# Hybrid diffusion layer on one core: one activation table for the attention, gate columns as native strips, other ranks in the written-out order

## The chip, the cores and the metric

The kernel runs on one core of a Trainium2 chip. The number that counts is device microseconds (us) of one launch, as the median of several runs. Four engines compute: TensorE (PE, matrix products into PSUM banks), VectorE (DVE), ScalarE (ACT) and GpSimd (POOL, which here only clears buffers and issues some DMAs). SyncE (SP) issues the other DMAs. Each engine works through its own list of instructions in a fixed order and waits on semaphores.

## The reference

One layer over 256 latent tokens and 256 context tokens of width 2048, all in float32:

```python
hx = _rmsnorm(x, norm1_g) * (1.0 + sc1_x) + sh1_x        # and hc from ctx
zx = hx @ w_in + b_in ; zc = hc @ w_in + b_in            # columns: S5 | conv | q | k | v | o | 16 gates
s5_x = s5_mixer(...)         # diagonal state space model, both directions, gelu, gated by a sigmoid
ml_x = mlstm_mixer(...)      # 4 heads of 256, both directions; gates: log_i, log_sigmoid(f)
cv_x = conv_module(...)      # depthwise convolution of 31 taps, layernorm, silu
x = x + g1_x * (concat([s5_x, cv_x, ml_x]) @ w_out)
hx2 = _rmsnorm(x, norm2_g) * (1.0 + sc2_x) + sh2_x
x = x + g2_x * ((silu(hx2 @ w_g) * (hx2 @ w_u)) @ w_ffn_out)
return _rmsnorm(x, norm_f_g)
```

The shifts, scales and gates (`sh`, `sc`, `g`) come from `silu(c) @ w_mod`, a matrix-vector product over 2048 x 12288 weights. In the attention part, each head and direction needs exponentials of a 256 x 512 block, and the readout needs `1/sqrt(var + eps)` per head, made from a logarithm and an exponential.

## The kernel before

**Weights.** All large matrices stream from memory in chunks of 8 tiles of 128 x 128 (`raw`, 512 KB, issued on SP's queue). Each chunk is split for fp32r products: ScalarE casts it to a high part (`split`: `whi`, line 577), VectorE subtracts to get the low part (`wlo`, line 579). Each of the three buffers has three places. An activation is split the same way (`hx`, `hc`, each with a high and a low half), and a product is three matmuls (`mm3`: high x high, high x low, low x high).

**Stages of TensorE's stream.** S5 and first K columns while the normalised input is made (to about 145 us), conv columns, the 16 gate columns, the other K columns, V columns (two blocks, `cb` 0 and 1, each ending in four additions that take the four PSUM banks to `vx`, line 1358), Q, O, the S5 gate (`glu`), the output projection in two halves, then the feed-forward part. In the V stage a block needs four banks for its whole length, and the three `ps_m` banks are all there are of that kind, so the next stage's first matmul waits for the first addition of the block before.

**Side work.** Generators (`s5_job`, `conv_job`, `mod_job`, `gates_job`, `attention`) are advanced between tiles by a small scheduler, `Sched`, so that their instructions are written between the matmuls. `mod_job` makes the second to last parts of the modulation with 512 KB weight pieces (`wm`) from POOL's queue, mostly as multiply-adds on VectorE (`macc`, line 489), each group of 16 ended by four transposes on TensorE. `s5_moves` (line 1094) copies the S5 columns `zT` into another partition order, `U`, with 8 copies on ScalarE and 8 on VectorE. It is called when the first stage ends.

**The order.** After everything is written, `Arrange` simulates all instructions with costs of its own and lays down a fixed order for each engine: whenever an engine is free it takes, of the instructions that are ready, the one with the lowest rank. A rank is the position in the order of writing, less what `ranks` holds for it (line 320). So rank only decides among instructions that are ready together, and its times are the costs written in `account`, not the chip's. Up to `strict`, TensorE keeps the order of writing.

**Activation tables.** ScalarE holds one table at a time, and a load is put before an activation whose function the table lacks. `lnexp()` (line 622) loads the one that has both logarithm and exponential. It is called for the first norm, the conv norm, the gates and two more norms, and not for the attention. `Arrange` counts Exp and Ln as one table, 1.

**Gates.** `load_gates` (line 662) loads 16 columns for each of 16 row tiles, splits them into high and low (`wgs`, 32 columns), and `gates_job` (line 1271) makes 64 fp32r matmuls that write 32 PSUM partitions. A product with `selg` then adds the high and the low rows and puts each group of four on its own 32 partitions.

Of the kernel before, what the change touches and what calls it, by code (L numbers as in the profile page):

```python
# [39 lines left out]
PUMP_EVERY = 8  # L40
URGENT = 0
S5_Y = (3000, 0, 0, 0)
# [109 lines left out]
class Arrange:  # L152
# [5 lines left out]
           "EngineType.SP": "SP"}  # L158
    SETS = {"Exp": 1, "Ln": 1, "Silu": 2, "Sigmoid": 3, "Sin": 4, "Gelu_apprx_tanh": 5}
    CALM, LATE, LATE_M = 140e3, 800.0, 0.0  # L160
    SEM, SAME, DMA, RATE = 45.0, 36.0, 1900.0, 345.0

# [112 lines left out]
    def account(self, k, i, e, size):  # L275
        n = max([s[0] for s in size] or [0])
        out = [s for s in size if s[4]]
        op, c = i.opcode, 0.0
        scal = sum(1 for x in size[:-1] if x[0] == 1)
        psum = any("_pp_" in self.tag.get(x[1], "") for x in size if not x[4])  # L280
        tab = None
        if op == "DMACopy":
            c = out[0][0] * out[0][3][0][1] * 4 / self.RATE
        elif e == "PE":
            cols = out[0][0]
            f32r = "float32r" in str(size[0][2])
            strip = i.tile_size[1] < 128
            c = 6 + 0.4427 * cols if f32r else 109.0 if i.is_transpose else 2 * max(0.8438 * cols, 110.0)
            if any(x[1].startswith(("whi", "wlo")) for x in size):
                self.main.add(k)  # L290
            self.mm[k] = (strip and not f32r, i.tile_position[1])
        elif e == "DVE":
            text = i.concise()
            c = 150 + (2.0 if "is_tensor_tensor_scan=True" in text else 0.5 if op == "Memset" else 1.05) * n
            c += 60 * scal
        elif op == "LoadActFuncSet":
            tab = 1
        elif e == "ACT":
            text = i.concise() if op == "Activation" else ""
            c = 190 + 0.84 * n + 95 * scal - (40 if op == "TensorCopy" and psum else 0)  # L300
            for f, s in self.SETS.items():
                if f"func=ActivationFunctionType.{f} " in text + " ":
                    tab = s
        else:
            c = 300.0
        self.cost.append(c)
        self.tab.append(tab)

    def run(self):
# [31 lines left out]
        while todo:  # L341
# [46 lines left out]
            if self.ins[k].opcode == "DMACopy":  # L388
                clock[e] = s + (530.0 if e == "POOL" else 60.0)
                pipe = max(s + self.DMA + (1200.0 if e == "POOL" else 0.0), pipe) + c  # L390
                done = pipe
# [15 lines left out]
            else:  # L407
                if self.tab[k] is not None and self.tab[k] != table:
                    table = self.tab[k]
                    s += 1300  # L410
# [42 lines left out]
def hybrid_layer_kernel(ctx: ExitStack, tc: tile.TileContext, xt, ctxt, wm1, wmr, wst, wg, bvrow, pvd, cstd, s5p, out):  # L453
# [20 lines left out]

    def tt(o, a, b, op, first=0):
        i = V.tensor_tensor(out=o, in0=a, in1=b, op=op)  # L476
        if first:
            ranks[i.ins.name] = first
        sc.dve += 62 + 1.05 * n_of(o)

    def ts(o, a, s1, op0, s2=None, op1=None):
# [6 lines left out]
    def stt(o, a, s, b, op0, op1):  # L488
        V.scalar_tensor_tensor(o, a, s, b, op0=op0, op1=op1)  # L489
        sc.dve += 62 + 1.05 * n_of(o)  # L490

    def vcopy(o, a):
        V.tensor_copy(o, a)
        sc.dve += 62 + 0.8 * n_of(o)

    def rsum(o, a):
# [7 lines left out]
    def act(o, a, f, bias=0.0, scale=1.0, pin=False):  # L504
        i = S.activation(o, a, f, bias=bias, scale=scale)  # L505
        if pin:
            keep(i)
        sc.act += 190 + 0.84 * n_of(o)

    def acopy(o, a, first=0):  # L510
        i = S.copy(o, a)  # L511
        if first:
            ranks[i.ins.name] = first
        sc.act += 190 + 0.84 * n_of(o)

    def mm(o, l, r, start, stop, native=False, tp=None, sgc=False, pin=False):
# [58 lines left out]
    def split(c):  # L575
        his[c] = sb.tile([128, CH * 128], F32R, name="whi", tag="whi", bufs=3)
        acopy(his[c], raw[c], URGENT)
        los[c] = sb.tile([128, CH * 128], F32R, name="wlo", tag="wlo", bufs=3)
        tt(los[c], raw[c], his[c], OP.subtract, URGENT)
        for d in (raw, his, los):  # L580
# [77 lines left out]
    for q in range(4):  # L658
        nc.sync.dma_start(cr[:, 4 * q:4 * q + 4, :], ctxt[:, 4 * q:4 * q + 4, :])
    wgs = pre.tile([128, KT, 32], F32R, name="wgs", tag="qh")  # L660

    def load_gates():
        wgr = tmp(256).rearrange("p (k n) -> p k n", k=KT)
        nc.sync.dma_start(wgr, wg)
        acopy(wgs[:, :, 0:16], wgr)
        tt(wgs[:, :, 16:32], wgr, wgs[:, :, 0:16], OP.subtract)

# [287 lines left out]
    csq = XB[:, 16 * ROWP + 1024:16 * ROWP + 2048].rearrange("p (t n) -> p t n", t=4)  # L955
    selg = XB[0:32, 3600:3728]
    nc.gpsimd.dma_start(selg, cstd[0:32, C_SELG:])
    V.memset(gp[:, :, :, 0:CONV_K // 2], 0.0)
# [135 lines left out]
    def s5_moves():  # L1094
        for s in range(4):
            for q in range(4):
                o = U[32 * s:32 * s + 32, q::4, :]
                i = zT[32 * q:32 * q + 32, :, s::4]
                if (s + q) % 2:
                    vcopy(o, i)  # L1100
                else:
                    acopy(o, i)

# [167 lines left out]
    def gates_job():  # L1271
        ps = bbank()
        for i, h in ((0, hx), (1, hc)):
            for kt in range(KT):
                for s in range(2):
                    mm(ps[0:32, 256 * i:256 * i + 256], wgs[:, kt, :], h[:, kt, s, :], kt == 0 and s == 0,
                       kt == KT - 1 and s == 1)
        rows = pre.tile([128, 1024], F32, name="rows", tag="qh")
        e = rows[0:32, 512:1024]
        acopy(e, ps[0:32, :])  # L1280
        yield 1500
# [61 lines left out]
    for cb in range(2):  # L1343
# [13 lines left out]
        for t in range(4):  # L1357
            tt(vx[:, t, 2 * cb:2 * cb + 2, 0:256], pss[t].rearrange("p (h d) -> p h d", h=2),
               bvb.rearrange("p (h d) -> p h d", h=2), OP.add)

# [76 lines left out]

    def attention():
        for h in range(ML_H):
            while st["tile"] < q_ready[h]:  # L1440
# [46 lines left out]
    for ct in range(4):  # L1487
# [3 lines left out]
        sg, f = tmp(256), tmp(256)  # L1491
        act(sg, ps[:, 0:256], AF.Sigmoid, bias=pvc("bglu", ct))
        tt(f, gT[ct // 2][:, ct % 2, :], sg, OP.mult)
        to_mix(mixs[:, ct], f)
    need_mod(0)
    rj = sc.add(readout(), 0)
    for ct in range(KT):
        ps = mbank()
        for i in range(8):
            src, j = (mx["c"], i) if i < 4 else (mixs, i - 4)  # L1500
            mm3(ps[:, 0:256], nxt(), (src[:, j, 0, :], src[:, j, 1, :]), i == 0, i == 7)
        stt(xres[:, ct, :], ps[:, 0:256], mods[:, 0, ct:ct + 1], xres[:, ct, :], OP.mult, OP.add)
    sc.finish(rj)
# [4 lines left out]
    class SumSq:  # L1508
# [7 lines left out]
        def add(self, x):  # L1516
            if self.n % 2 == 0:
                self.t = tmp(512)
            sq = self.t[:, 256 * (self.n % 2):256 * (self.n % 2) + 256]
            act(sq, x, AF.Square)  # L1520
            self.sq.append(sq)
# [17 lines left out]
    for ct in range(KT):  # L1539
        ps = mbank()  # L1540
        for i in range(8):
            mm3(ps[:, 0:256], nxt(), (mixm[:, i, 0, :], mixm[:, i, 1, :]), i == 0, i == 7)
        stt(xres[:, ct, :], ps[:, 0:256], mods[:, 0, ct:ct + 1], xres[:, ct, :], OP.mult, OP.add)
        if ct == 14:
# [98 lines left out]
def pack(inp):  # L1643
# [24 lines left out]
    g = f["w_in"][0][:, OFF_G:][:, gi]  # L1668
    a["wg"] = np.ascontiguousarray(g.reshape(KT, 128, 16).transpose(1, 0, 2))
    bi = f["b_in"][0]  # L1670
# [41 lines left out]
    cst[:, C_MR:C_MR + 128] = np.tril(np.ones((128, 128)))  # L1712
    for r in range(32):
        q = r % 16
# [34 lines left out]
```

## Time and profile before

| | us |
|---|---|
| median of 3 runs | 1461.62 (1460.66 to 1464.09) |
| the profiled execution, its own time | 1460.26 |
| its span, first to last instruction | 1458.5 |
| TensorE busy | 1412.2 (97%) |
| VectorE busy | 1050.6 (72%) |
| ScalarE busy | 751.1 (52%) |
| mean granted TensorE clock | 0.989 of full |

Between the span and the execution's own time lie 1.8 us. Busy matmul time has modelled ends, so 97% doesn't say that TensorE works at its peak. It says that little of the span is left in which it waits for somebody.

### The profile page before, as it was taken

How to read it: one execution, taken by the hardware profiler on the slowest of the kernel's cores; microseconds unless marked ns; L12 is line 12 of the kernel's file. 1: busy time of each engine (PE TensorE's matmuls, PEld its weight loads, DVE VectorE, ACT ScalarE, POOL GpSimd, SP SyncE). 2: the span in 40 equal slices, each digit the busy share in tenths (PEclk: the TensorE clock that was granted, in tenths of full speed). 3: DMA queues.
4: the chain of work that ended last, by engine and by line, in shares of the span. 5: the costliest groups of instructions: out<-in, count | busy, mean ns of one | idle time of the engine just before them, and what ended most of it. 6: DMA issues, size and time to landing. Idle time of an engine off the chain costs nothing.

```text
span 1458.5 us, 25393 instructions
## 1 busy us (share of the span) xinstructions
PE 1412.2 (97%) x9856; PEld 1242.8 (85%) x9856; DVE 1050.6 (72%) x1945; ACT 751.1 (52%) x1311; POOL 108.2 (7%) x207
## 2 busy tenths in 40 slices
PE   6999899999999999999999999999999999999996
PEld 4888788887788999998998888888888888888885
DVE  8555699997878787888877778566555665556665
ACT  5334886665664555545555545533444334444353
POOL 1221111110001001011000010000000000000000
PEclk9999999999999999999999999999999999999998
DMA  9997553453428467689477787555555555555553
GB/s 369 366 356 288 180 204 129 177 190 106 158 73 309 169 239 255 228 303 332 146 252 271 270 297 256 185 189 186 188 188 188 188 186 188 188 188 188 188 174 115
DMA packets 87928, 315.31 MB, mean 216 GB/s; under 512 B 10096, under 2 KB 10880, under 8 KB 87808
## 3 DMA queue, kind: packets, MB, share of 16 engines
q1 hardware_dynamic: 60912, 216.67, 42.9%
q0 software_dynamic: 26896, 97.02, 18.6%
q8 instruction: 77, 1.26, 0.3%
q14 instruction: 43, 0.35, 0.1%
HBM read 311.55 MB, written 2.10 MB: 215 GB/s over the span
## 4 chain that ended last, share of the span: by engine, by line
PE 72%; issue 18%; DMA 4%; DVE 2%; POOL 2%; ACT 1%; SPq 0%; POOLq 0%; DVEq 0%
PE ps_m L520 45%; PE ps_qk L520 19%; PE ps_b L520 8%; DMA wm<-in_wmr_dram 4%; POOL wm L650 1%; DVE tmp L476 0%; ACT U L511 0%; ACT tmp L505 0%; PE ps_b L1163 0%; DVE xres L476 0%; PE ps_b L1070 0%; DMA xr<-in_xt_dram 0%; DVE wlo L476 0%; DVE tmp L489 0%; DVE macc L489 0%
## 5 line engine op out<-in xcount | busy, mean ns | idle before, releaser
L476 DVE TENSOR_TENSOR wlo<-raw,whi 128x1024 fp32r<-128x1024 f32 x386 | 471.7, 1223 | 267.4 <-ACT whi L511 262.4
L511 ACT CAST whi<-raw 128x1024 fp32r<-128x1024 f32 x386 | 403.9, 1047 | 456.5 <-PE ps_m L520 248.1
L520 PE MATMUL ps_m<-h,whi 128*128 128x512 f32 (+1 forms) x800 | 252.4, 369 | 3.5 <-ACT h L505 3.5
L520 PE MATMUL ps_m<-ffa,whi 128*128 128x512 f32 x704 | 249.0, 396 | 0.0
L520 PE MATMUL ps_qk<-h,whi 128*128 128x512 f32 (+1 forms) x688 | 233.0, 383 | 0.0
L520 PE MATMUL ps_m<-h,wlo 128*128 128x256 f32 x704 | 199.8, 284 | 0.0
L520 PE MATMUL ps_m<-ffa,wlo 128*128 128x256 f32 x704 | 198.7, 282 | 0.0
L520 PE MATMUL ps_m<-hx,whi 128*128 128x256 f32 x960 | 187.4, 290 | 6.4 <-ACT hx L505 3.2
L520 PE MATMUL ps_qk<-h,wlo 128*128 128x256 f32 x656 | 185.5, 283 | 0.0
L520 PEld LDWEIGHTS ps_m<-h,whi 128*128 128x128 f32 x800 | 145.1, 190 | 30.4 <-ACT h L505 3.9
L520 PEld LDWEIGHTS ps_m<-hx,whi 128*128 128x128 f32 x960 | 149.4, 190 | 21.5 <-issue 16.5
L520 PEld LDWEIGHTS ps_m<-ffa,whi 128*128 128x128 f32 x704 | 132.3, 188 | 32.2 <-issue 1.2
L520 PEld LDWEIGHTS ps_qk<-h,whi 128*128 128x128 f32 x688 | 127.3, 188 | 27.1
L489 DVE SCALAR_TENSOR_TENSOR macc<-wm,cs,macc 128x512 f32<-128x512 f32 x180 | 134.4, 747 | 11.3 <-DMA wm<-in_wmr_dram 7.4
L520 PE MATMUL ps_m<-hx,wlo 128*128 128x256 f32 x480 | 136.8, 285 | 0.7 <-DVE wlo L476 0.7
L520 PEld LDWEIGHTS ps_m<-h,wlo 128*128 128x128 f32 x704 | 133.2, 189 | 0.0
L520 PEld LDWEIGHTS ps_m<-ffa,wlo 128*128 128x128 f32 x704 | 132.3, 188 | 0.1
L520 PEld LDWEIGHTS ps_qk<-h,wlo 128*128 128x128 f32 x656 | 123.4, 188 | 0.0
L650 POOL DMA_DIRECT2D wm<-in_wmr_dram x128 | 67.8, 531 | 602.9 <-DVE macc L489 428.5
L489 DVE SCALAR_TENSOR_TENSOR xres<-ps_m,mods,xres 128x256 f32<-128x256 f32 x160 | 77.0, 482 | 33.6 <-PE ps_m L520 31.6
L520 PEld LDWEIGHTS ps_m<-hx,wlo 128*128 128x128 f32 x480 | 91.3, 190 | 1.4 <-DVE wlo L476 1.2
L489 DVE SCALAR_TENSOR_TENSOR XB<-XB,pv 128x256 f32<-128x256 f32 x120 | 53.8, 475 | 0.4
(273 smaller groups left out, 2134.2 us busy)
## 6 DMA issues: line engine op xcount, KB each, us to landing
raw<-in_wst_dram SPq DMA_DIRECT2D x386, 512.0 KB, 4.2
wm<-in_wmr_dram POOLq DMA_DIRECT2D x128, 512.0 KB, 5.2
wm<-in_wm_dram POOLq DMA_DIRECT2D x24, 512.0 KB, 7.2
wmu<-in_wm_dram POOLq DMA_DIRECT2D x16, 512.0 KB, 7.3
wmt<-in_wm_dram POOLq DMA_DIRECT2D x8, 512.0 KB, 7.7
wms<-in_wm_dram POOLq DMA_DIRECT2D x7, 512.0 KB, 6.2
xr<-in_xt_dram SPq DMA_DIRECT2D x4, 512.0 KB, 5.7
cr<-in_ctxt_dram SPq DMA_DIRECT2D x4, 512.0 KB, 8.9
```

Of the source, the lines that this page charges most:

```text
L476: i = V.tensor_tensor(out=o, in0=a, in1=b, op=op)
L489: V.scalar_tensor_tensor(o, a, s, b, op0=op0, op1=op1)
L511: i = S.copy(o, a)
L520: i = P.matmul(o, lhsT=l, rhs=r, start=start, stop=stop, skip_group_check=sgc, **kw)
L650: i = (q or nc.gpsimd).dma_start(wm[key], src)
```

## The change

1. **Table.** `attention` calls `lnexp()` at its first step. In `Arrange`, Exp is now known to lie in tables 1 and 7, Ln in 6 and 7, and the preloaded table is 7.
2. **Gates.** `wgs` is loaded as plain float32 with 32 columns, of which 16 are zero, straight into its place. The cast, the subtraction and a temporary buffer go. The 64 matmuls are native float32, in groups of four side by side: each writes its own 32 of 128 PSUM partitions and takes every fourth row tile. `selg` has 128 rows and adds the four strips.
3. **Ranks.** `split` (`U_SPLIT`), the two places with `U_OUT`, and `U_GLU` have 0, which is what they had. `s5_moves` gets -60 (`U_MOVE`): each of the 16 copies ranks as if written 60 instructions later. The `vx` additions get 1000 (`U_V`): as if written 1000 instructions earlier.

```diff
-URGENT = 0
+U_SPLIT, U_MOVE, U_V, U_OUT, U_GLU = (0, -60, 1000, 0, 0)
...
-    SETS = {"Exp": 1, "Ln": 1, "Silu": 2, "Sigmoid": 3, "Sin": 4, "Gelu_apprx_tanh": 5}
+    SETS = {"Exp": (1, 7), "Ln": (6, 7), "Silu": (2,), "Sigmoid": (3,), "Sin": (4,), "Gelu_apprx_tanh": (5,)}
...
-            tab = 1
+            tab = (7,)
...
-                if self.tab[k] is not None and self.tab[k] != table:
-                    table = self.tab[k]
+                if self.tab[k] is not None and table not in self.tab[k]:
+                    table = self.tab[k][0]
                     s += 1300
...
+    def ahead(n, i):
+        ranks[i.ins.name] = n
...
-        acopy(his[c], raw[c], URGENT)
+        ahead(U_SPLIT, acopy(his[c], raw[c]))
...
-    wgs = pre.tile([128, KT, 32], F32R, name="wgs", tag="qh")
+    wgs = pre.tile([128, KT, 32], F32, name="wgs", tag="qh")
 
     def load_gates():
-        wgr = tmp(256).rearrange("p (k n) -> p k n", k=KT)
-        nc.sync.dma_start(wgr, wg)
-        acopy(wgs[:, :, 0:16], wgr)
-        tt(wgs[:, :, 16:32], wgr, wgs[:, :, 0:16], OP.subtract)
+        nc.sync.dma_start(wgs, wg)
...
-    selg = XB[0:32, 3600:3728]
-    nc.gpsimd.dma_start(selg, cstd[0:32, C_SELG:])
+    selg = XB[:, 3600:3728]
+    nc.gpsimd.dma_start(selg, cstd[:, C_SELG:])
...
                 if (s + q) % 2:
-                    vcopy(o, i)
+                    ahead(U_MOVE, vcopy(o, i))
                 else:
-                    acopy(o, i)
+                    ahead(U_MOVE, acopy(o, i))
...
-            for kt in range(KT):
+            for k in range(0, KT, 4):
                 for s in range(2):
-                    mm(ps[0:32, 256 * i:256 * i + 256], wgs[:, kt, :], h[:, kt, s, :], kt == 0 and s == 0,
-                       kt == KT - 1 and s == 1)
+                    for j in range(4):
+                        mm(ps[32 * j:32 * j + 32, 256 * i:256 * i + 256], wgs[:, k + j, :], h[:, k + j, s, :].bitcast(F32),
+                           k + s == 0, k == KT - 4 and s == 1, native=True, tp=(0, 32 * j), pin=i + k + s + j > 0)
         rows = pre.tile([128, 1024], F32, name="rows", tag="qh")
-        e = rows[0:32, 512:1024]
-        acopy(e, ps[0:32, :])
+        e = rows[:, 512:1024]
+        acopy(e, ps)
...
-            tt(vx[:, t, 2 * cb:2 * cb + 2, 0:256], pss[t].rearrange("p (h d) -> p h d", h=2),
-               bvb.rearrange("p (h d) -> p h d", h=2), OP.add)
+            ahead(U_V, tt(vx[:, t, 2 * cb:2 * cb + 2, 0:256], pss[t].rearrange("p (h d) -> p h d", h=2),
+                          bvb.rearrange("p (h d) -> p h d", h=2), OP.add))
...
     def attention():
+        lnexp()
         for h in range(ML_H):
```

## Rows read from the trace of the kernel before

**Rows 1.** The page's first part: busy us, share of the span, instructions.
```profile
PE 1412.2 (97%) x9856; PEld 1242.8 (85%) x9856; DVE 1050.6 (72%) x1945; ACT 751.1 (52%) x1311; POOL 108.2 (7%) x207
```

**Rows 2.** Waits of TensorE, whole span: total us, times, longest us.
```profile
PE ps_m L520 <- DVE vx L476: 5.1, 2, 3.2
```

**Rows 3.** Stretches: length, busy us by engine, granted TensorE clock (PEclk), DMA.
```profile
156.10:160.30 4.20, 3.62 (x18) 3.39 (x19) 3.60 (x4) 4.16 (x10) 0.00 (x0) 0.59 0.40 124
...
380.70:385.20 4.50, 4.45 (x21) 3.92 (x21) 4.37 (x9) 4.06 (x13) 0.00 (x0) 0.65 0.13 32
...
443.30:447.10 3.80, 3.80 (x22) 3.80 (x21) 3.80 (x6) 0.80 (x1) 0.53 (x1) 0.55 0.63 221
...
450.00:575.00 125.00, 125.00 (x882) 117.05 (x882) 98.58 (x232) 68.31 (x135) 12.72 (x24) 1.00 0.67 232
```

**Rows 4.** ScalarE in order of time at the S5 copies: start, us.
```profile
145.90 1.25 ACT L505 ACTIVATE kT<-ps_b,bks 128x512 f32<-128x512 f32 x2
147.16 7.86 ACT L511 COPY U<-zT 32x512 f32<-32x512 f32 x7
155.04 1.99 ACT L511 CAST whi<-raw 128x1024 fp32r<-128x1024 f32 x2
```

**Rows 5.** TensorE in order of time, same place.
```profile
151.63 0.40 PE L520 MATMUL ps_b<-hx,whi 128*128 128x256 f32 x2
...
151.99 0.40 PE L520 MATMUL ps_b<-hx,whi 128*128 128x256 f32 x2
...
156.14 0.50 PE L520 MATMUL ps_b<-hx,whi 128*128 128x256 f32 x2 [3.64 <-ACT whi L511]
...
157.40 0.58 PE L520 MATMUL ps_b<-hx,wlo 128*128 128x256 f32 x1 [0.54 <-DVE wlo L476]
```

**Rows 6.** VectorE, end of the first V block.
```profile
380.00 0.69 DVE L476 TENSOR_TENSOR vx<-ps_m,bvb 128x512 f32<-128x512 f32 x1
```

**Rows 7.** TensorE, end of the first V block.
```profile
376.35 0.62 PE L520 MATMUL ps_m<-whi,hx 128*128 128x512 f32 x2
...
380.75 0.51 PE L520 MATMUL ps_m<-whi,hx 128*128 128x512 f32 x1 [1.91 <-DVE vx L476]
```

**Rows 8.** VectorE, end of the second V block.
```profile
437.57 1.22 DVE L476 TENSOR_TENSOR wlo<-raw,whi 128x1024 fp32r<-128x1024 f32 x1
439.86 1.54 DVE L489 SCALAR_TENSOR_TENSOR macc<-wm,cs,macc 128x512 f32<-128x512 f32 x2 [1.06 <-DMA wm<-in_wmr_dram]
441.31 1.28 DVE L476 TENSOR_TENSOR vx<-ps_m,bvb 128x512 f32<-128x512 f32 x2
```

**Rows 9.** TensorE, end of the second V block.
```profile
442.14 0.47 PE L520 MATMUL ps_m<-hx,whi 128*128 128x256 f32 x2 [3.17 <-DVE vx L476]
```

**Rows 10.** TensorE: the gate matmuls, and strips of the first stage's modulation.
```profile
96.08 0.64 PE L520 MATMUL ps_b<-wmt,cs 128*32 128x256 f32 x8
...
96.97 1.05 PE L520 MATMUL ps_b<-wm,cs 128*32 128x256 f32 x16
...
220.79 3.80 PE L520 MATMUL ps_b<-hx,wgs 128*32 128x256 f32 x32
224.43 3.79 PE L520 MATMUL ps_b<-hc,wgs 128*32 128x256 f32 x32
```

**Rows 11.** ScalarE's groups, 450 to 580 us: busy, mean ns, idle before.
```profile
L505 ACT ACT_TABLE_LOAD x9 | 11.5, 1283 | 0.2
```

**Rows 12.** ScalarE in order of time: table loads around the second head's norm.
```profile
512.64 0.30 ACT L505 ACTIVATE tmp<-mvv,kc 128x2 f32<-128x2 f32 x1 [1.08 <-DVE mvv L1430]
512.96 1.28 ACT L505 ACT_TABLE_LOAD   x1
```

**Rows 13.** VectorE: the last modulation groups of the second scale, and its first use.
```profile
663.01 0.16 DVE L476 TENSOR_TENSOR mods<-mods,pv 128x4 f32<-128x4 f32 x1 [0.33 <-ACT macc L1076]
...
688.48 0.17 DVE L489 SCALAR_TENSOR_TENSOR A<-mods,pv 128x16 f32<-128x16 f32 x1
...
694.19 0.41 DVE L485 TENSOR_SCALAR tmp<-tmp,A,mods 128x256 f32<-128x256 f32 x1
```

More of the change, by code (lines that the diff above doesn't have):

```diff
@@ L158 @@
            "EngineType.SP": "SP"}
-    SETS = {"Exp": 1, "Ln": 1, "Silu": 2, "Sigmoid": 3, "Sin": 4, "Gelu_apprx_tanh": 5}
+    SETS = {"Exp": (1, 7), "Ln": (6, 7), "Silu": (2,), "Sigmoid": (3,), "Sin": (4,), "Gelu_apprx_tanh": (5,)}
     CALM, LATE, LATE_M = 140e3, 800.0, 0.0
-    SEM, SAME, DMA, RATE = 45.0, 36.0, 1900.0, 345.0
+    SEM, SAME, DMA, RATE, SOFT = 45.0, 36.0, 1900.0, 345.0, 1200.0
     def __init__(self, tc, pins, ranks, strict):
@@ L389, in run @@
                 clock[e] = s + (530.0 if e == "POOL" else 60.0)
-                pipe = max(s + self.DMA + (1200.0 if e == "POOL" else 0.0), pipe) + c
+                pipe = max(s + self.DMA + (self.SOFT if e == "POOL" else 0.0), pipe) + c
                 done = pipe
@@ L473, in n_of, with tt @@
         return n
[L475 to L478, printed above, removed]
+    def tt(o, a, b, op):
         sc.dve += 62 + 1.05 * n_of(o)
+        return V.tensor_tensor(out=o, in0=a, in1=b, op=op)
     def ts(o, a, s1, op0, s2=None, op1=None):
@@ L488, in stt @@
     def stt(o, a, s, b, op0, op1):
-        V.scalar_tensor_tensor(o, a, s, b, op0=op0, op1=op1)
         sc.dve += 62 + 1.05 * n_of(o)
+        return V.scalar_tensor_tensor(o, a, s, b, op0=op0, op1=op1)
     def vcopy(o, a):
-        V.tensor_copy(o, a)
         sc.dve += 62 + 0.8 * n_of(o)
+        return V.tensor_copy(o, a)
     def rsum(o, a):
@@ L508, in act, with acopy @@
         sc.act += 190 + 0.84 * n_of(o)
[L510 to L513, printed above, removed]
+        return i
+    def acopy(o, a):
         sc.act += 190 + 0.84 * n_of(o)
+        return S.copy(o, a)
+    def ahead(n, i):
+        ranks[i.ins.name] = n
     def mm(o, l, r, start, stop, native=False, tp=None, sgc=False, pin=False):
@@ L576, in split @@
         his[c] = sb.tile([128, CH * 128], F32R, name="whi", tag="whi", bufs=3)
-        acopy(his[c], raw[c], URGENT)
+        ahead(U_SPLIT, acopy(his[c], raw[c]))
         los[c] = sb.tile([128, CH * 128], F32R, name="wlo", tag="wlo", bufs=3)
-        tt(los[c], raw[c], his[c], OP.subtract, URGENT)
+        ahead(U_SPLIT, tt(los[c], raw[c], his[c], OP.subtract))
         for d in (raw, his, los):
@@ L1491, in hybrid_layer_kernel @@
         sg, f = tmp(256), tmp(256)
-        act(sg, ps[:, 0:256], AF.Sigmoid, bias=pvc("bglu", ct))
-        tt(f, gT[ct // 2][:, ct % 2, :], sg, OP.mult)
-        to_mix(mixs[:, ct], f)
+        ahead(U_GLU, act(sg, ps[:, 0:256], AF.Sigmoid, bias=pvc("bglu", ct)))
+        ahead(U_GLU, tt(f, gT[ct // 2][:, ct % 2, :], sg, OP.mult))
+        ahead(U_GLU, acopy(mixs[:, ct, 0, :], f))
+        ahead(U_GLU, tt(mixs[:, ct, 1, :], f, mixs[:, ct, 0, :], OP.subtract))
     need_mod(0)
@@ L1501, in hybrid_layer_kernel @@
             mm3(ps[:, 0:256], nxt(), (src[:, j, 0, :], src[:, j, 1, :]), i == 0, i == 7)
-        stt(xres[:, ct, :], ps[:, 0:256], mods[:, 0, ct:ct + 1], xres[:, ct, :], OP.mult, OP.add)
+        ahead(U_OUT, stt(xres[:, ct, :], ps[:, 0:256], mods[:, 0, ct:ct + 1], xres[:, ct, :], OP.mult, OP.add))
     sc.finish(rj)
@@ L1519, in add @@
             sq = self.t[:, 256 * (self.n % 2):256 * (self.n % 2) + 256]
-            act(sq, x, AF.Square)
+            ahead(U_OUT, act(sq, x, AF.Square))
             self.sq.append(sq)
@@ L1542, in hybrid_layer_kernel @@
             mm3(ps[:, 0:256], nxt(), (mixm[:, i, 0, :], mixm[:, i, 1, :]), i == 0, i == 7)
-        stt(xres[:, ct, :], ps[:, 0:256], mods[:, 0, ct:ct + 1], xres[:, ct, :], OP.mult, OP.add)
+        ahead(U_OUT, stt(xres[:, ct, :], ps[:, 0:256], mods[:, 0, ct:ct + 1], xres[:, ct, :], OP.mult, OP.add))
         if ct == 14:
@@ L1668, in pack @@
     g = f["w_in"][0][:, OFF_G:][:, gi]
-    a["wg"] = np.ascontiguousarray(g.reshape(KT, 128, 16).transpose(1, 0, 2))
+    a["wg"] = np.zeros((128, KT, 32), np.float32)
+    a["wg"][:, :, 0:16] = g.reshape(KT, 128, 16).transpose(1, 0, 2)
     bi = f["b_in"][0]
@@ L1712, in pack @@
     cst[:, C_MR:C_MR + 128] = np.tril(np.ones((128, 128)))
-    for r in range(32):
+    for r in range(128):
         q = r % 16
```

## The prediction

> **What bounds the kernel now.** I read the page first. TensorE is busy 1412.2 of 1458.5 us [rows 1], so a change of the order can win only where TensorE stands still or runs slowly: some 46 us of idle time, a good part of it at the two ends. Then the waits of TensorE. The costliest that the change touches is the one for `vx`, 5.1 us in two pieces [rows 2]. Then the timelines around the S5 copies and around the ends of the two V blocks, which show what stood in the way [rows 4 to 9], and the stretches behind these waits, which show what followed [rows 3]. Each of the three waits is followed by some 4 us at a granted clock of 0.59, 0.65 and 0.55, that is, mostly at the lower of the two levels, 1.2 instead of 2.4 GHz. A stretch of length L at clock c loses (1 - c) x L: 1.72, 1.58 and 1.71 us. So each wait costs its length and about 1.6 to 1.7 us more.
>
> **The S5 copies (U_MOVE, a gain of 2.5 us).** A conv chunk lasts 8 products of 0.36 us, 2.9 us [rows 5]. Chunk 16 should start at 152.34, 0.36 after the last triple of chunk 15. It starts at 156.14: TensorE waited 3.64 us for the cast, and 0.54 more for the low part. ScalarE had been making the S5 copies, seven of them in 7.86 us, 1.12 us each, and made the cast only after them [rows 4]. With the slow stretch the place costs 3.64 + 0.54 + 1.72 = 5.9 us. The planner didn't see it: its formula, 190 + 0.84 x 512, gives 620 ns for a copy.
>
> Will a rank 60 later cure this? In the order of writing, the copies are instructions 1486 to 1501 and the casts of chunks 15, 16 and 17 are 1503, 1530 and 1567 (counted in the code). With 60 more, the copies rank 1546 to 1561. So the cast of chunk 16 now goes ahead, as soon as its buffer is free, which is when the first stage ends, about 145.5. The cast of chunk 17 still ranks behind all copies. ScalarE's work from 145.9 is then 1.25 for K, about 1.0 for the cast and the copies as before, so the copies end at about 156.05 instead of 155.04, and the cast of chunk 17 ends at 157.1. Chunk 16 runs from 152.34 to 155.2. TensorE then waits 1.9 us for the cast, and, the low part taking 1.22 us more [rows 8], about another 1.0 after its first two matmuls. It is through the first product of chunk 17 at about 158.6. Before, that product ended near 161.7 (156.14, five triples by 160.3, four more of 0.36). That is 3.1 us. If the slow stretch comes again at its full cost, 1.8. I take 2.5. Bounds: 0, if the cast is not pulled forward, to 5.9, if the stall goes whole. The copies themselves end 1 us later; their first reader, an S5 product, comes after 170 us, so nothing waits for them.
>
> **The vx additions (U_V, 8.4 us).** First block: the bank's last matmul starts by 376.35 [rows 7], and the addition starts at 380.00 [rows 6], behind small S5 operations that were written earlier and so ranked first. TensorE waits 1.91 us, then the slow stretch costs 1.58: 3.5 us. With 1000 off, the additions (instructions 4170 to 4173 and 4460 to 4463) rank before all S5 work, written up to 4144. VectorE is free at about 377.6, after the subtraction that it has begun. The addition takes 0.69 and the bank is free at 378.3, before TensorE's next matmul is due at about 378.8, the 380.75 less the wait. The other three follow every 0.6 us, faster than TensorE asks for banks. So the whole 3.5 goes. Second block: the same, with `macc` in front. VectorE finishes a subtraction at 438.79, waits 1.06 us for a weight piece, makes two `macc` and only then adds [rows 8]. TensorE waits 3.17 [rows 9] and loses 1.71 in the slow stretch: 4.9 us. The bank is full some 2 us before TensorE needs it, as in the first block, that is by 437, so the addition can go before those two `macc`. Together 8.4; bounds 3.5 (the second addition still behind a `macc` that waits for its piece) to 8.4. What is late in their place: the S5 operations and `macc` by up to 2.6 us, four additions of 0.65. Their readers are the S5 gate near 580 and the modulation, of which more below.
>
> **The gates (0.2 us).** Before, 64 matmuls in 2 x 3.64 = 7.3 us, start to start [rows 10]. After, 16 groups of four. The modulation strips of the first stage are the same operation, the same tile and length; each float32 matmul shows as two records, so 16 records, two groups, take 96.97 - 96.08 = 0.89 us [rows 10], and 16 groups take 7.1. A gain of 0.2, bounds -0.3 and 0.6. The cast, the subtraction and the temporary buffer that go lie in a stretch where neither engine sets the pace: nothing. The copy of the result has 512 elements per partition as before.
>
> **The table (nothing).** From 450 to 580 us ScalarE loads a table nine times, 1.28 us each [rows 11]. One remains: eight loads, 10.3 us of ScalarE's time. What hides them is TensorE's own work: it is busy for all 125 us of that stretch at full clock, and ScalarE only 68 [rows 3]. So nothing on the path. If that cover were gone, up to 10.3. The planner counted no load in the attention before, nor does it now, so its order doesn't change by this.
>
> The Trainium skill, "ScalarE: Activation LUTs", section "What ACT_TABLE_LOAD costs", gives 1283 ns for the load and a drain of about 1380 ns, 2.66 us for each switch. The trace agrees with the load and not with the drain: the activation before it ends at 512.94 and the load starts at 512.96 [rows 12]. By the page the eight would be 21 us, an estimate, and still hidden.
>
> **The sum.** 2.5 + 8.4 + 0.2 = 11.1 us from 1460.26, the profiled execution's own time, gives 1449.2. The median of the runs is 1.4 higher, so on its scale **1450.5**, and I say 1450. A new order also moves other instructions about; I know no sign for that and give it 3 us either way.
>
> **The rivals.**
> - *The copies give nothing* (the stall moves by one chunk at its old cost): 8.6 less, 1453. For it: chunk 17 stays behind the copies. Against it: a whole chunk is done meanwhile. 0.14.
> - *The copies' stall goes whole*: 14.5 less, 1447. Against it: the count of instructions. 0.08.
> - *The second addition stays late*, because `macc` waits for its piece before it: 11.1 - 4.9 = 6.2 less, 1455.5. For it: the 1.06 us wait [rows 8]. 0.08.
> - *The modulation takes part back.* The second scale `A` is ready at 688.65, and the first use is at 694.19, so there are 5.5 us of slack [rows 13]. If its chain doesn't come forward with TensorE, all but 5.5 of the gain is waited away: 1456. Against it: each group's transposes sit in TensorE's order, and the chain moves with it. 0.05.
> - *The same chain turns the sign.* A group ends about 25 us after the one before, 663.01 and 688.48 [rows 13]. If a group's start slips behind the next transposes, the scale comes up to 25 us late: 25 - 5.5 = 20 us of wait against 11 won, 1470. It decides from a slip of 5.5 + 11.1 = 16.6 us on. 0.06.
> - *The ranks change nothing that matters*, since they act only among instructions ready together in the planner's own time, or new stalls of the new order eat the gain: 1460 to 1461. 0.05.
> - *The tables were on the path*: 10.3 more, 1440. By the waits there is nothing for it. 0.02.
>
> The Trainium skill, "ScalarE: Activation LUTs", section "Rules for kernel authors", asks to budget about 2.7 us for every switch. Read as time of the whole kernel, that is this last case at the page's price, 21 us, an estimate; no wait of TensorE in the trace bears it out.
>
> **How the numbers follow.** The forecast has 0.52, with its own range of 1446 to 1454. The range of 1445 to 1458 takes in all cases but the sign change, no change and the tables, 0.13, and the tails of the others. Faster or slower counts from 0.2%, 2.9 us, about what a measurement of this kernel can tell. Faster: 0.52 + 0.14 + 0.08 + 0.08 + 0.05 + 0.02, less 0.03 for tails, 0.86. Same: 0.05 and the tails, 0.08. Slower: 0.06.
>
> **What would show it.** In the profile after: no wait of TensorE for `vx`, and the clock at 1.00 after both V blocks. Between the S5 copies on ScalarE stands one cast, the wait at 152 has shrunk and lies one chunk later, about 2 to 3 us in two pieces. The gate group lasts 7.1 us. ScalarE loads eight tables fewer, and one alone from 430 to 575 us. The first use of `A` comes some 11 us earlier, without a wait for it. Wrong would make it: a long wait of TensorE anywhere that was not there before, above all for a `macc` or for `h` near 685; a cast of chunk 16 that still follows the copies; or `vx` additions behind a `macc`.

## The result, and the profile after

The changed kernel takes 1447.20 us (median of four runs, 1446.73 to 1447.81), the kernel before, timed beside it, 1462.86. The ratio is 0.9894, with a 95% interval of 0.9877 to 0.9911. Timed once more later (E5 below), it took 1445.92 against 1457.47, 0.9921 (0.9901 to 0.9941). So the change wins 11.6 to 15.7 us, and the forecast of 1450, 11.1 us less than before, lies close by. Its terms fit less well than its sum, as the profile shows.

The profiled execution after lasted 1447.56 us, with a span of 1445.8 at a mean clock of 0.993. The first part of its page (busy us, share of the span, instructions), to be held against [rows 1]:

```profile
PE 1404.1 (97%) x9920; PEld 1234.9 (85%) x9920; DVE 1049.0 (73%) x1944; ACT 738.3 (51%) x1302; POOL 107.7 (7%) x207
```

TensorE has 64 more instructions and 8 us less busy time. Some 6 us of that are time not spent at the slow clock, an estimate from the two mean clocks (1458.5 x 0.011 before, 1445.8 x 0.007 after). ScalarE has lost 12.8 us. The waits of TensorE after (total us, times, longest us), of which the one for `vx` answers to [rows 2]; from the others those are taken that the text speaks of:

```profile
PE ps_b L1067 <- DVE macc L488: 3.1, 3, 1.4
...
PE ps_m L520 <- DVE vx L477: 2.0, 1, 2.0
...
PE ps_b L520 <- ACT whi L511: 1.7, 1, 1.7
PE ps_b L520 <- DVE wlo L477: 0.8, 1, 0.8
```

One wait for `vx` is left of two. The waits for `macc`, 3.1 us, are new: before, the only one of them from 440 us on was 0.3 us.

**The S5 copies.** ScalarE in order of time (start, us), answering to [rows 4]:

```profile
146.72 1.03 ACT L511 CAST whi<-raw 128x1024 fp32r<-128x1024 f32 x1
147.78 7.89 ACT L511 COPY U<-zT 32x512 f32<-32x512 f32 x7
155.69 1.04 ACT L511 CAST whi<-raw 128x1024 fp32r<-128x1024 f32 x1
```

TensorE there, answering to [rows 5], and then the stretch behind it (length, busy us, granted clock, DMA), to [rows 3]:

```profile
156.78 0.50 PE L520 MATMUL ps_b<-hx,whi 128*128 128x256 f32 x2 [1.68 <-ACT whi L511]
...
158.04 0.53 PE L520 MATMUL ps_b<-hx,wlo 128*128 128x256 f32 x1 [0.75 <-DVE wlo L477]
```

```profile
156.70:161.30 4.60, 3.76 (x17) 0.66 0.46 132
```

One cast has gone ahead, the seven copies follow, and the wait comes one chunk later in two pieces. The slow stretch came again: 4.60 x (1 - 0.66) = 1.6 us.

**The V blocks.** VectorE at the end of the first one, to [rows 6], and then of the second, to [rows 8]:

```profile
370.29 1.22 DVE L499 TENSOR_TENSOR_SCAN Vr<-WR,Vr 128x512 f32<-128x512 f32 x1
371.42 0.67 DVE L477 TENSOR_TENSOR vx<-ps_m,bvb 128x512 f32<-128x512 f32 x1
...
425.68 1.29 DVE L477 TENSOR_TENSOR gs<-gT,gs 128x512 fp32r<-128x512 f32 x2 [3.42 <-ACT gs L511]
...
427.66 1.22 DVE L477 TENSOR_TENSOR wlo<-raw,whi 128x1024 fp32r<-128x1024 f32 x1 [0.61 <-ACT whi L511]
428.81 0.74 DVE L488 SCALAR_TENSOR_TENSOR macc<-wm,cs,macc 128x512 f32<-128x512 f32 x1
429.47 1.22 DVE L477 TENSOR_TENSOR wlo<-raw,whi 128x1024 fp32r<-128x1024 f32 x1
430.60 1.88 DVE L477 TENSOR_TENSOR vx<-ps_m,bvb 128x512 f32<-128x512 f32 x3
```

TensorE at the end of the second block, to [rows 9]:

```profile
431.43 0.47 PE L520 MATMUL ps_m<-hx,whi 128*128 128x256 f32 x2 [1.98 <-DVE vx L477]
```

In the first block the addition follows the operation that VectorE has begun, and TensorE doesn't wait. In the second, VectorE had stood still for 3.42 us for the cast of `gs` on ScalarE, as it had in the kernel before, and then made the two subtractions of `gs`, two low parts and a `macc`, and the addition comes 2 us late.

**Gates, tables, modulation.** TensorE's gate groups, to [rows 10]; ScalarE's group of table loads from 450 to 580 us, to [rows 11]; VectorE at the second scale and its first use, to [rows 13]:

```profile
216.00 3.66 PE L520 MATMUL ps_b<-hx,wgs 128*32 128x256 f32 x64
219.48 3.64 PE L520 MATMUL ps_b<-hc,wgs 128*32 128x256 f32 x64
222.94 1.04 PE L520 MATMUL ps_b<-wm,cs 128*32 128x512 f32 x8
```

```profile
L503 ACT ACT_TABLE_LOAD x1 | 1.3, 1283 | 0.0
```

```profile
676.94 0.17 DVE L488 SCALAR_TENSOR_TENSOR A<-mods,pv 128x16 f32<-128x16 f32 x1
682.65 0.41 DVE L483 TENSOR_SCALAR tmp<-tmp,A,mods 128x256 f32<-128x256 f32 x1
```

The gates take 222.94 - 216.00 = 6.94 us, one table load is left, and `A` is ready at 677.11, 11.5 us earlier than before and 5.5 ahead of its first use, as before.

Where the time came from is read by setting the same instruction of both traces side by side. TensorE's first gate group starts 4.8 us earlier than before, its first product behind the second V block 442.14 - 431.43 = 10.7. Taken along the products with a low part, in order, the lead of the changed kernel (its usual value in a stretch) is 0.2 us at 145, 1.7 at 180, 2.0 at 205, 4.9 at 218, 5.6 at 231, 9.5 behind the first V block, 12.2 behind the second, and 12.7 at the end. So the copies gave 1.4, the V blocks 3.9 and 2.7. Between 180 and 231 us came 3.9, of which the gates and the selection behind them are 0.7; the rest no step of the prediction had. Behind the V blocks 1.5 go again by 460 us, at the first of the waits for `macc`, and 1.8 come back near 585 us, where the kernel before waits 1.2 and 0.4 us for ScalarE.

The largest part of the 3.9 lies at a late piece of the modulation's weights in the profiled execution before. TensorE before, at that place, and then after:

```profile
205.53 1.05 PE L520 MATMUL ps_b<-wm,cs 128*32 128x512 f32 x4
208.46 1.05 PE L520 MATMUL ps_b<-wm,cs 128*32 128x512 f32 x4 [1.87 <-DMA wm<-in_wmr_dram]
209.44 0.51 PE L520 MATMUL ps_m<-hx,whi 128*128 128x256 f32 x2
```

```profile
205.83 1.06 PE L520 MATMUL ps_b<-wm,cs 128*32 128x512 f32 x8
```

The eight records of such a group take 1.0 us from start to start elsewhere and took 3.9 here: 2.9 us lost.

### The profile page after: what moved, and what is told of

It reads as the page before. It is cut to its first block, busy times and chain, and to the rows that moved or that the text cites. A ratio compares the mean times of both kernels' runs of the same rounds, so it can differ in the third digit from the quotient of the medians.

```text
span 1445.8 us, 25513 instructions
## 1 busy us (share of the span) xinstructions
PE 1404.1 (97%) x9920; PEld 1234.9 (85%) x9920; DVE 1049.0 (73%) x1944; ACT 738.3 (51%) x1302; POOL 107.7 (7%) x207
## 4 chain that ended last, share of the span: by engine, by line
PE 74%; issue 14%; DMA 4%; DVE 3%; POOL 2%; ACT 2%; SPq 0%; POOLq 0%; DVEq 0%; ACTq 0%
PE ps_m L520 48%; PE ps_qk L520 18%; PE ps_b L520 8%; DMA wm<-in_wmr_dram 2%; POOL wm L650 1%; DVE macc L488 1%; DMA wmu<-in_wm_dram 1%; DVE wlo L477 1%; DMA wmt<-in_wm_dram 1%; DMA cr<-in_ctxt_dram 1%; ACT whi L511 1%; DMA raw<-in_wst_dram 0%; ACT U L511 0%; POOL wmu L650 0%; PE ps_b L1160 0%
## 5 line engine op out<-in xcount | busy, mean ns | idle before, releaser
L520 PEld LDWEIGHTS ps_m<-hx,whi 128*128 128x128 f32 x960 | 148.2, 189 | 20.3 <-issue 15.3
```

Of the source, the lines that this page charges most:

```text
L520: i = P.matmul(o, lhsT=l, rhs=r, start=start, stop=stop, skip_group_check=sgc, **kw)
```

## The experiments

The kernel before was timed beside each of them. E1 to E4 were timed together, E5 to E8, and E9 to E11; E12 alone. The difference is median against median of the same group, and the last column is the profiled execution's own time. The intervals of the ratios are 3.5 to 6 us wide, so differences of a microsecond or two are read from the profiles, one execution each.

| kernel | us | difference | ratio, 95% | profiled |
|---|---|---|---|---|
| changed, first time | 1447.20 | -15.7 | 0.9894 (0.9877-0.9911) | 1447.56 |
| E1 vx additions as before | 1448.31 | -10.9 | 0.9926 (0.9909-0.9944) | 1448.04 |
| E2 copies' rank as before | 1451.89 | -7.4 | 0.9951 (0.9939-0.9963) | 1451.63 |
| E3 tables as before | 1447.69 | -11.6 | 0.9923 (0.9909-0.9936) | 1449.87 |
| E4 gates as before | 1447.68 | -11.6 | 0.9922 (0.9908-0.9935) | 1450.36 |
| E5 changed, again | 1445.92 | -11.6 | 0.9921 (0.9901-0.9941) | 1444.83 |
| E6 copies 120 later | 1450.28 | -7.2 | 0.9948 (0.9928-0.9969) | 1451.18 |
| E7 same, right price | 1448.22 | -9.3 | 0.9937 (0.9917-0.9956) | 1448.00 |
| E8 before + vx | 1452.93 | -4.5 | 0.9965 (0.9951-0.9980) | 1451.20 |
| E9 before + copies' rank | 1453.25 | -7.1 | 0.9959 (0.9947-0.9972) | 1453.25 |
| E10 12 copies on VectorE | 1445.03 | -15.3 | 0.9899 (0.9884-0.9913) | 1445.42 |
| E11 same, price of gT | 1443.39 | -16.9 | 0.9893 (0.9878-0.9909) | 1442.88 |
| E12 E11 again | 1442.30 | -16.7 | 0.9886 (0.9869-0.9903) | 1440.64 |

**E1: the additions' rank taken back.**

```diff
-U_SPLIT, U_MOVE, U_V, U_OUT, U_GLU = (0, -60, 1000, 0, 0)
+U_SPLIT, U_MOVE, U_V, U_OUT, U_GLU = (0, -60, 0, 0, 0)
```

> The changed kernel with the priority of the four vx additions of each V block taken back (1000 to 0); all else as changed. Theory: the two V blocks give what the alignment of the two traces shows, 3.9 us in the first and 2.7 in the second, so this kernel is 6.6 us slower than the changed one, with a wait for vx of about 1.9 us at the end of the first block and 3.2 at the end of the second, each with a slow clock behind it. Rival A: the additions gave all of the predicted 8.4, and something else took 1.8 back; then it is 8.4 slower. Rival B: the gain came with the shift of the whole order and not from the additions; then it is within 1 us of the changed kernel.

The theory fell. Against E5 the loss is 0.6 us by the differences, within what these runs can tell, and that is rival B's number. TensorE at the ends of its two V blocks:

```profile
376.97 0.50 PE L520 MATMUL ps_m<-whi,hx 128*128 128x512 f32 x1 [1.12 <-DVE vx L477]
...
434.01 0.47 PE L520 MATMUL ps_m<-hx,whi 128*128 128x256 f32 x2 [2.03 <-DVE vx L477]
```

The first wait is back, shorter than before. The second is as long without the priority as with it, 2.03 against 1.98. Along the products E1 is 2.5 us behind the changed kernel after both blocks, but 1.1 of that it had lost at a late weight piece near 261 us, where its order is still that of the changed kernel. By 650 us it is level again: it has none of the 3.1 us of waits for `macc`. Whether all 3.1 belong to the priority isn't settled, since E5, the changed kernel itself, had only 0.8 of them from 440 us on.

**E2: the copies' rank taken back.**

```diff
-U_SPLIT, U_MOVE, U_V, U_OUT, U_GLU = (0, -60, 1000, 0, 0)
+U_SPLIT, U_MOVE, U_V, U_OUT, U_GLU = (0, 0, 1000, 0, 0)
```

> The changed kernel with the S5 copies at their old rank (-60 to 0). Theory: the stall at 152 us comes back as it was, 1.4 us; the wait of 1.87 us for a weight piece of the modulation that stood at 208 us before was a meeting of two transfers and may come back with the old times, 2.9 us from start to start: 1.4 to 4.3 us slower than the changed kernel. Rival A: the rank itself is worth the predicted 2.5 and nothing else hangs on it: 2.5 slower. Rival B: the rank is worth nothing: within 0.5 us.

It is 4.2 us slower than the changed kernel by the differences, the upper end of the theory. The profile has the wait of 3.6 us at 156, the late weight piece (a wait of 0.35; the eight records take 2.4 us from start to start in place of 1.0), and a second `vx` wait of 3.0 in place of 2.0: 2.3 us behind before the end of the second block, 4.1 at the end.

**E3: the old tables in the new order.** Only the table that is loaded ahead of the attention is another one; the order of every engine stays.

```diff
     def attention():
-        lnexp()
+        keep(S.preload_act_table_set("exp_and_others"))
```

> The changed kernel with its order of instructions on every engine, but the table loaded ahead of the attention is the one with the exponential alone, so ScalarE loads a table again at each logarithm and at each exponential behind one: eight loads more, 10.3 us of ScalarE's time. Theory: TensorE's own work covers them, so the time stays within 0.7 us. Rival A: the loads are on the path at their own 1.28 us: 10.3 slower. Rival B, by the Trainium skill's price for a switch: 21 slower, an estimate.

No loss against E5 by the differences, and both rivals are out. By the profiled executions it is 2.3 us longer than the first one of the changed kernel, so a loss of a microsecond or two can't be excluded. The profile has waits of TensorE for ScalarE near 571 and 575 us that neither execution of the changed kernel has, in the same order of every engine:

```profile
PE ps_m L520 <- ACT tmp L503: 1.2, 1, 1.2
PE ps_m L520 <- ACT RH L503: 0.3, 1, 0.3
```

The kernel before (1.2 and 0.4), E8 and E9, all with the old tables, have this pair as well; of the kernels with the new tables only E4 has it. So the table may be worth some 1.5 us there. It is not shown: E4 speaks against it, and ScalarE's casts ahead of that place wait for late weights in E3 (2.55 us for one), which may be chance. A third wait of 1.2 us, at 667, E3 has alone. ScalarE's group and its order around one pair of loads:

```profile
L503 ACT ACT_TABLE_LOAD x9 | 11.5, 1283 | 0.2
```

```profile
501.53 0.30 ACT L503 ACTIVATE tmp<-mvv,kc 128x2 f32<-128x2 f32 x1 [1.12 <-DVE mvv L1428]
501.85 1.28 ACT L503 ACT_TABLE_LOAD   x1
503.14 0.21 ACT L503 ACTIVATE tmp<-tmp 128x2 f32<-128x2 f32 x1
```

The load stands right behind one activation and right ahead of the next. The Trainium skill, "ScalarE: Activation LUTs", section "What ACT_TABLE_LOAD costs", adds a drain of about 1380 ns to its 1283; the trace has the 1283 and no drain, here as before [rows 12].

**E4: the old gates.**

```diff
-            for k in range(0, KT, 4):
+            for kt in range(KT):
                 for s in range(2):
-                    for j in range(4):
-                        mm(ps[32 * j:32 * j + 32, ...], wgs[:, k + j, :], ..., native=True, tp=(0, 32 * j), ...)
+                    mm(ps[0:32, 256 * i:256 * i + 256], wgs[:, kt, :], h[:, kt, s, :], ...)
```

Its weights are again cast and split, and the selection matrix has 32 rows.

> The changed kernel with the gates as they were: float32r matmuls of 32 columns, the weights cast and split, and the selection matrix on 32 rows. Theory: the new gates are worth 0.4 us in the 64 or 128 matmuls and 0.4 in the selection behind them, as the traces show, so this is 0.4 to 0.9 us slower. Rival A: the old gates' load, cast and subtraction are what let the weight piece of the modulation come late at 208 us: then 3 to 4 us slower, with that wait in the profile. Rival B: nothing to measure, within 0.3 us.

No difference from E5 that can be measured. The old gates didn't cause the late weight piece: this kernel has them and not the wait.

**E5: the changed kernel again.** No edit.

> The changed kernel once more, beside the three that follow, so that they have a neighbour on the same chip. Expected: 0.989 of the kernel before, as in its first runs (0.9877 to 0.9911), and the same waits of TensorE in the profile.

The ratio is above the expected interval, but the two intervals overlap (0.9901 to 0.9911). The waits at 156 and 431 us are the same (1.7, 0.8, 2.0). The `macc` waits are not: 0.8 in place of 3.1 us. Its execution is 2.7 us shorter than the first, and that lead arises between 600 and 680 us.

**E6: the copies 120 later.**

```diff
-U_SPLIT, U_MOVE, U_V, U_OUT, U_GLU = (0, -60, 1000, 0, 0)
+U_SPLIT, U_MOVE, U_V, U_OUT, U_GLU = (0, -120, 1000, 0, 0)
```

> The changed kernel with the S5 copies ranked 120 later in place of 60, so that they rank 1606 to 1621, behind the casts of chunks 16 and 17 (1530 and 1567). Theory: what is left at 152 to 161 us in the changed kernel, waits of 1.7 and 0.8 and 1.7 lost to the slow clock, 4.1 us, comes from the one cast that still ranks behind the copies; it goes, and the kernel is 3 to 4 us faster than the changed one. Rival A: the planner prices a copy at 0.62 us where it takes 1.12, so a cast planned in time is late all the same, and the stall moves by a chunk: within 1 us. Rival B: the first S5 products wait for the copies: slower by 1 to 4.

The theory fell: 4.4 us slower than E5 by the medians. The wait at 156 is gone, and in its place TensorE waits at 167, then 1.2 us for a weight piece:

```profile
167.24 1.24 PE L520 MATMUL ps_b<-Mb,WR 128*32 128x128 f32 x32 [3.63 <-DVE XB L488]
```

VectorE's `XB` had waited for ScalarE, which made the last two copies, casts and two table loads ahead of it. So the stall is at a bank that VectorE frees late, and TensorE waits neither for a cast nor for a copy, as the rivals had it. Length, busy us of TensorE, its weight load, VectorE, ScalarE and GpSimd, granted clock and DMA, from 150 to 168 us, first in the changed kernel, then in E6:

```profile
150.00:168.00 18.00, 15.57 (x139) 13.84 (x138) 7.22 (x10) 17.63 (x27) 1.63 (x4) 0.91 0.55 178
```

```profile
150.00:168.00 18.00, 14.00 (x139) 12.58 (x139) 7.47 (x10) 17.77 (x26) 2.11 (x4) 0.99 0.57 206
```

ScalarE is busy for 17.6 of 18 us there, and VectorE for 7.2. If ScalarE's work is the cause of the stall, a rank can only choose who is late; E10 tests that.

**E7: the same with the right price.**

```diff
-            c = 190 + 0.84 * n + 95 * scal - ...
+            c = 190 + (1.83 if size[0][3][0][1] == 32 else 0.84) * n + 95 * scal - ...
```

> As the kernel with the copies ranked 120 later, and the planner's price of ScalarE's copies on 32 partitions set to what the profile shows, 190 + 1.83 per element (1.12 us for 512, 0.42 for 128) in place of 190 + 0.84. Theory: with the right price no cast is planned behind a row of copies, so the stall at 152 to 161 us goes whole (4.1 us), and at the end of the second V block VectorE isn't held by a cast of gs that ScalarE has not made, so the 2.0 us wait for vx there shrinks to under 1: 4 to 6 us faster than the changed kernel. Rival: the order moves other waits about, and the macc transposes give it back as they did with the vx additions: within 2 us.

Half of it held by the profile. The second `vx` wait shrank to 0.2 us, as expected. The stall behind the copies stayed, 2.9 us for `XB`, and the kernel is 2.3 us slower than E5 by the medians, with intervals that overlap.

**E8 and E9: one rank alone, in the kernel before.** E8:

```diff
-               bvb.rearrange("p (h d) -> p h d", h=2), OP.add)
+               bvb.rearrange("p (h d) -> p h d", h=2), OP.add, 1000)
```

> The kernel before with the vx additions' priority alone (1000 for all eight). Theory: it gains what stood at the ends of the two V blocks, 3.5 and 4.9 us by the prediction's terms, but the macc additions that now come later make TensorE's transposes wait some 3 us further on, as the changed kernel does against the one with the additions at their old rank: 3 to 6 us faster than before. Rival A: the whole 8.4 stays. Rival B: all of it is given back: within 1.5 us of the kernel before.

4.5 us faster, inside the range, but not for its reason: no wait for `macc` came. The first block's wait is gone, and the second is 1.99 us. Up to the first V block this kernel has the order of the kernel before on every engine. Yet at the late weight piece it loses less:

```profile
204.96 2.09 PE L520 MATMUL ps_b<-wm,cs 128*32 128x512 f32 x8
206.98 0.51 PE L520 MATMUL ps_m<-hx,whi 128*128 128x256 f32 x2
```

The eight records take 2.0 us from start to start, 1.0 lost in place of 2.9, and no wait is counted. So 1.9 of the 2.9 were a chance of the one execution that was profiled. The other 1.0 seems to go with the order: with the copies' old rank some is lost there each time (2.9, 1.0 here, 1.4 in E2), with the rank of -60 and eight copies on each engine never (the changed kernel twice, E1, E3, E4, E9), and with -120 again 2.3 and 2.0 (E6, E7). E9:

```diff
                 if (s + q) % 2:
-                    vcopy(o, i)
+                    ranks[V.tensor_copy(o, i).ins.name] = -60
+                    sc.dve += 62 + 0.8 * n_of(o)
                 else:
-                    acopy(o, i)
+                    acopy(o, i, -60)
```

> The kernel before with the S5 copies' rank alone (-60). Theory: the rank does two things, it moves the stall at 152 by a chunk (1.4 us) and it changes the order on GpSimd's queue and the times of the modulation's weight pieces, so that the wait of 1.87 us for one at 208, 2.9 from start to start, is gone: 4 to 5 us faster than before. Rival A: the rank alone is worth the predicted 2.5, the weight piece comes late as before. Rival B: it carries more than 6 us, since the shift also helps the V blocks.

7.1 us faster by the medians, 4.1 to 7.7 by the interval. Theory and rival B each hold in part. Along the products E9 leads the kernel before by 1.5 us behind the copies. At the weight piece, which is in time, it gains 2.9 more, of which 1.9 are the chance that E8 showed; GpSimd's queue does have another order ahead of it, but whether that is the reason these runs don't show. It loses 1.0 again by 310 us, and the V blocks give 1.8 and 1.4: the first has no wait for `vx`, though the additions keep their old rank, since the first addition now comes before the small S5 operations that held it back, and the second has one of 1.81 us in place of 3.17.

**E10: 12 of the 16 copies on VectorE.**

```diff
-                if (s + q) % 2:
+                if (s + q) % 4:
                     ahead(U_MOVE, vcopy(o, i))
```

> The changed kernel with 12 of the 16 S5 copies on VectorE and 4 on ScalarE, in place of 8 and 8, the rank of -60 kept. Theory: what holds TensorE up at 152 to 168 us is ScalarE's work in that stretch, eight copies of 1.12 us among the casts, and a rank can only choose who is late; VectorE makes a copy in 0.62 and stands idle for 6.4 us there. With four copies less ScalarE wins 4.5 us, cast 17 ends near 152.5 in place of 156.7, and the waits of 1.7 and 0.8 and the 1.7 of slow clock behind them go: 3 to 4 us faster than the changed kernel. Rival A: the new order brings back a wait for a weight piece of the modulation or for a macc, 1 to 3 us, and nothing is left. Rival B: VectorE is late with the low part of chunk 16 or 17: within 1 us.

The two waits behind the copies, 1.7 and 0.8 us, are gone; two for `Wi` came, 0.8 and 0.5, and the clock stays at 1.00 from 140 to 250 us. The difference to the kernel before is -15.3 against -11.6 and -15.7 of the changed kernel. By its profile it is 2.1 us shorter than the changed kernel's first and 0.6 longer than E5. So the profile shows the stall gone once ScalarE has less work there, which answers E6, and the time doesn't show a gain.

**E11 and E12: the price of the gT copies as well.**

```diff
-            c = 190 + 0.84 * n + 95 * scal - ...
+            c = 190 + (1.83 if size[0][3][0][1] == 32 and n == 128 else 0.84) * n + 95 * scal - ...
```

> As the kernel with 12 copies on VectorE, and the planner's price of ScalarE's sixteen gT copies (32 partitions, 128 elements) set to the 0.42 us of the profile in place of 0.30. Theory: the cast of gs on ScalarE is then planned when it comes, VectorE makes the vx additions of the second V block ahead of it, and the wait of 2.0 us for vx there goes, as it went to 0.2 in the kernel with the price of all such copies: 1.5 to 2 us faster than the kernel with 12 copies. Rival: the macc additions behind them make TensorE's transposes wait by as much: within 0.7 us of it.

> The kernel with 12 copies on VectorE and the right price of the gT copies once more, since its first ratio (0.9893, 0.9878 to 0.9909) lies on one of the changed kernel's two (0.9894 and 0.9921) while its profile is 4.7 us shorter than the changed kernel's first. Theory: the stalls at 152 and 431 are gone, some 4 to 6 us, so 0.986 to 0.990 of the kernel before, and no wait over 1 us between 140 and 450 us. Rival: the gain of the profile was the chance of one execution: 0.990 to 0.993, with such waits.

E11 is 1.6 us faster than E10 by the medians, as expected, though their runs overlap; along the products it gains 2.2 us where the two orders part, at the end of the second V block. TensorE there, and the stretch of the copies (columns as for E6):

```profile
427.85 0.47 PE L520 MATMUL ps_m<-hx,whi 128*128 128x256 f32 x2 [0.16 <-DVE vx L477]
```

```profile
150.00:168.00 18.00, 17.21 (x168) 14.87 (x166) 13.95 (x22) 14.22 (x27) 2.65 (x5) 1.00 0.67 221
```

VectorE has taken over ScalarE's work, and TensorE is busy for 17.2 us in place of 15.6. From 140 to 450 us no wait of TensorE is over 0.8 us, in both executions. With 1443.39 and 1442.30 us, these runs lie below all of the changed kernel's (1444.83 to 1449.12), but they were not timed beside it: by the ratios, 0.9893 and 0.9886 stand against 0.9894 and 0.9921. It beats the kernel before by 16.7 to 16.9 us; against the changed kernel a gain of 1 to 5 us is likely and not settled to the microsecond.

## Why the prediction was right, and where it was not

**The sum.** 11.1 us were forecast and 11.6 to 15.7 measured, inside the range. Some of its agreement is luck, since terms missed on both sides.

**The copies (2.5).** The count of instructions was right: the cast of chunk 16 goes ahead, that of 17 stays behind, and the waits of 1.9 and 1.0 were 1.68 and 0.75. The slow stretch came again with 1.6 us, so the place gave 1.4, near the case of 1.8; 2.5 was the middle between that and no slow stretch. In E9 and E4 waits as long (1.9 and 0.8, 1.8 and 0.8) had no slow stretch behind them. What no step had: the rank also moves what stands at the ends of the V blocks. In E9 the first block's wait is gone by the copies' rank alone, in E8 by the additions' alone, though E1, with the copies' rank, has 1.1 of it. The second block's is 1.8 in E9, 2.0 in E8, and 2.0 with both. So at the V blocks the two terms are not a sum. The times don't settle it: alone the two are worth 7.1 and 4.5, which makes the 11.6 of E5, and taken back alone 4.2 and 0.6, each known to some 2 to 4 us.

**The additions (8.4).** The first block gave 3.9 for 3.5. The second gave 2.7 for 4.9, and here the step "the addition can go before those two `macc`" failed. The wait is 1.99 us with the priority in E8, 2.03 without it in E1, and 0.2 once the planner knows what a gT copy costs (E7, E11). The planner had the copies on ScalarE 0.12 us too cheap sixteen times, and so put work that VectorE then had to wait for ahead of the additions. With the right price the additions come before a low part and the `macc` (E7, where VectorE still waits 3.44 us for `gs`) or before the subtractions of `gs` (E11). The other 1.06 us of before were VectorE's own wait for a weight piece [rows 8], which in other orders stands behind the first addition (0.96 in E1, 1.18 in E9). Its slow stretch didn't come in the changed kernel.

**What is late instead.** The prediction let `macc` be late at no cost and looked for the cost at `h`. `A` came forward by 11.5 us with its slack whole, as it said. The `macc` transposes in TensorE's order did wait, 3.1 us in one execution and 0.8 in another. "A long wait that was not there before, above all for a `macc`" was named as what would make it wrong; it came, small.

**Gates (0.2) and table (0).** 7.36 became 6.94 us in the trace, near the 7.1; E4 can't tell it from nothing. Eight loads less on ScalarE are worth nothing that E3's times could measure, and 10.3 is excluded. The cover named, TensorE's own work, was there from 450 to 575 us in the kernel before; just behind that stretch, at 583 and 587 us, it has the two waits for ScalarE that E3 brings back, so up to some 1.5 us for the table stay open.

**What the sum didn't know.** It was made against one execution, and in that one 2.9 us were lost at a late weight piece. By E8, 1.9 of them were chance and no gain of the change. The other 1.0 is lost in none of the six profiled executions with the copies at -60, eight on each engine, and the prediction had no term for it. So of the 12.7 us between the two profiles some 2 are luck, and the rest is near the 11.1 because the copies (1.1 short) and the second V block (2.2 short) were made up by gains that no step had.

## What to carry to other kernels

Where a stall stands behind a row of operations, take the busy share of their engine in that stretch first: if it is full, as ScalarE was for 17.6 of 18 us, a priority only moves the stall, and work must move to the engine that stands idle. Two edits that act on the same wait are no sum: take each back alone and make each alone before their gains are added, and read the wait itself, since the times may not tell. And ask of each wait for a transfer what a second execution of the same order has there: here 2.9 us were lost in one and 1.0 in the other.

## What the runs showed of the hardware

Two waits of the same length at the same place, in front of the same products, were followed by different clocks. In the changed kernel TensorE stood 1.98 us and went on at full clock; in E8 it stood 1.99 us and then fell to half. The stretch behind the wait in the first, then the wait and the stretch in the second (length, busy us, granted clock, DMA):

```profile
431.40:433.40 2.00, 1.97 (x16) 1.00 0.94 315
433.40:435.40 2.00, 2.00 (x19) 1.00 0.63 250
```

```profile
434.33 0.48 PE L520 MATMUL ps_m<-hx,whi 128*128 128x256 f32 x2 [1.99 <-DVE vx L476]
434.30:436.30 2.00, 1.97 (x15) 0.89 0.79 240
436.30:438.30 2.00, 2.00 (x11) 0.50 0.91 365
```

So a wait's price may include a slow stretch or not (1.6 to 1.7 us where it did), and the length of the wait alone doesn't say which: at this place waits of 1.8 to 2.0 us had one behind them in E1, E6, E8 and E9, and none in the changed kernel, E3, E5 and E10. The prediction had it go with the wait. What decides it these runs don't show.

In the changed kernel ScalarE takes 1.12 us for a strided copy of 512 elements on 32 partitions (`U` from `zT`) and 0.42 for one of 128 (`gT` from `U`), that is some 0.18 us and 1.83 ns for each element; VectorE takes 0.62 and 0.27 for its share of the same copies.
